# A diffusion transformer block: token tiles loaded into slots, small constants issued from GpSimd, projections three tiles behind

## The chip, the core and the metric

The kernel runs on one core of a Trainium2 chip. The metric is the device time of one execution in microseconds (us); lower is better. The engines are TensorE (PE, with its weight loads PEld), VectorE (DVE), ScalarE (ACT), GpSimd (POOL) and SyncE (SP). SP computes nothing: it issues the transfers between the chip's memory and SBUF. Each engine takes its instructions in the order in which they are written for it, and waits at one whose inputs or buffer are not there yet.

## The reference

One block of a diffusion transformer in float32, with 1024 tokens and 256 context tokens of 1024 features. Six modulation vectors come from a condition vector; attention is over a neighbourhood of 8 x 16 tokens of a 16 x 64 grid plus all context tokens. Cut to what runs:

```python
sh1, sc1, g1, sh2, sc2, g2 = adaln(c, w_mod, b_mod)        # silu(c) @ w_mod + b_mod, in six parts
csh1, csc1, ... = adaln(c_ctx, w_mod, b_mod)
h  = modulate(rms_norm(x,  norm1), sh1,  sc1)              # h * (1 + scale) + shift
hc = modulate(rms_norm(ctx, norm1), csh1, csc1)
q = rms_norm(split_heads(h @ w_q), q_gain)
k = rms_norm(split_heads(h @ w_k), k_gain);   v  = split_heads(h @ w_v)
kc = rms_norm(split_heads(hc @ w_k), k_gain); vc = split_heads(hc @ w_v)
y = neighbourhood_attention(q, k, v, kc, vc, rpb) @ w_o
x = x + g1 * y
x = x + g2 * conv_ffn(modulate(rms_norm(x, norm2), sh2, sc2), w_up, conv_w, conv_b, w_down)
```

## The kernel before

All matrix products that matter are done in a split form: each operand is a rounded part (names ending in h) and a remainder (names ending in l), and three matmuls stand for one product. ACT or DVE makes the rounded part, DVE or POOL subtracts to get the remainder.

The tokens are held in ten tiles of 128 rows and 1024 columns (512 KB): tiles 8 and 9 are the context, 0 to 7 the tokens. A token tile takes eight neighbouring rows out of every 64 rows of x. `TORD` is the order 8, 9, 0, 1, ... 7.

The start, which the change is about, has these steps.

- **Modulation (L240 to L270).** Four segments of w_mod, for scale and shift of the first norm, come as 16 pieces of 512 KB (`mraw`, `load_m`). ACT rounds each (`mh`, L246), DVE makes the remainder (`ml`, L247), PE multiplies (`pm`, L257 and L258). After four pieces ACT copies the sum out (`mrow`, L262), and PE turns it into columns with the small constant `comb` (`pc`, L264). After the eighth piece DVE makes the scale `s1` (L267, L268), after the sixteenth the shift `b1` (L270), with the constants `bcol` and `n1c`.
- **Loads of tokens (`load_x`).** They go into four buffers named `pt`, of which three first hold pieces of w_mod and which the attention uses later. So a fifth tile is loaded only when an earlier one has been transposed.
- **Per tile, `stats_x`:** ACT squares the rows and sums them (L155; the squares themselves are put into `htl`, where nobody reads them), DVE and POOL make the inverse root (`ss`, L156 and L157), DVE scales the tile (L176).
- **Per tile, `transpose_x`:** PE transposes eight blocks of 128 x 128 into PSUM (L182, three buffers), DVE and ACT apply scale and shift to four blocks each (`hv`, L189 and L191), ACT makes `hth` (L193), and DVE or POOL `htl` (L194).
- **Weights of the first pair of heads (`load_w`, `prep_w`):** four transfers `wr` of 384 KB, eight casts `wh` on DVE (L144), eight remainders `wl` on POOL (L147).
- **Projections (`qkv_gen`, L301, L303, L305):** 24 matmuls per tile into one of two PSUM buffers `pq`. The rows are then squared and normalised (L322 to L325) and copied out as `v`, `q` and `kn` (L329 to L340). The `kn` instruction is the last reader of the buffer; the tile after next waits for it.

The later parts of the modulation vectors are computed a little at a time by DVE from transfers `mr` of 128 KB with two buffers (`macc`, L469 and L471), beside the attention of eight pairs of heads. Then follow the output projection and the feed-forward part.

What sets the order: the program is written in the order that the code shows, and a scheduler then lists the instructions of each engine in an order of its own making, with its own estimate of durations. The order of the code decides which of several ready instructions comes first. `AHEAD` in the loop of L549 says by how many tiles the projections follow the transpositions in the code.

All transfers issued by SP share eight completion counters in turn. A transfer is issued only when the one eight places earlier has landed.

`big` is a region of slots under tags; the order list of L118 says which slots hold `hth` and `htl` of which tile.

## Time and profile before

| | us |
|---|---|
| time, median of 3 runs | 1489.94 (1489.22 to 1491.38) |
| profiled execution: span from the first to the last instruction (no other time is listed for it) | 1491.8 |
| PE busy | 1386.5 (93%) |
| DVE busy | 1208.1 (81%) |
| POOL busy | 805.7 (54%) |
| ACT busy | 738.1 (49%) |

The span of the profiled execution is 1.9 us above the median of the runs. In the rows of the profile, each instruction has its start and duration, its engine, its line, what it writes and reads, and in brackets the idle time of its engine before it and what ended that. Rows by group give a count, the sum and the mean of the durations, then the idle time ahead of the group. A row in order of time may merge several equal instructions (x4). A row named SPq is the issue of a transfer, not the transfer.

### The profile page before, as it was taken

What the parts mean: (1) busy time and instruction counts of PE and PEld (TensorE: products, weight loads), DVE (VectorE), ACT (ScalarE), POOL (GpSimd) and SP (SyncE); (2) the same over time, 40 slices, a digit from 0 to 9 for tenths busy, and PEclk for the clock granted to TensorE, in tenths of its full rate; (3) what the DMA queues carried; (4) which work ended last, traced back from release to release, by engine and by line L of the source; (5) the groups of instructions that cost most, each with busy time, mean ns of one, the idle gap of its engine ahead of it and who ended that gap; (6) DMA issues with size and microseconds to landing.
All of it is one profiled execution on the core that took longest, in us unless ns stands there. A gap on an engine that the chain in (4) does not pass through costs nothing.

```text
span 1491.8 us, 22077 instructions
## 1 busy us (share of the span) xinstructions
PE 1386.5 (93%) x7396; PEld 1200.0 (80%) x7396; DVE 1208.1 (81%) x2392; ACT 738.1 (49%) x1601; POOL 805.7 (54%) x672
## 2 busy tenths in 40 slices
PE   6689999999999999999996999999999987898998
PEld 2589889898989899888885777888888865686887
DVE  6778878888888878866589889788877779988884
ACT  6575645555565656645465434344343334244541
POOL 1455544545454546744368545555545568474872
PEclk9899999999999999999997999999999998899999
DMA  9612221313131202262132132233332347433343
GB/s 315 161 37 60 64 87 55 92 51 103 49 101 45 77 14 73 69 152 76 50 129 99 64 108 101 96 106 106 107 106 99 106 137 286 155 100 127 110 131 105
DMA packets 84827, 153.27 MB, mean 103 GB/s; under 512 B 9945, under 2 KB 49001, under 8 KB 84713
## 3 DMA queue, kind: packets, MB, share of 16 engines
q1 hardware_dynamic: 84712, 151.86, 32.7%
q8 instruction: 58, 0.95, 0.3%
q14 instruction: 57, 0.46, 0.1%
HBM read 119.05 MB, written 32.78 MB: 102 GB/s over the span
## 4 chain that ended last, share of the span: by engine, by line
PE 60%; DVE 20%; DMA 7%; POOL 5%; issue 4%; ACT 3%; SPq 0%; DVEq 0%; POOLq 0%; ACTq 0%
PE pg L740 8%; PE pa L740 7%; PE sw L740 6%; PE pq L301 5%; PE pq L303 5%; PE pq L305 5%; DMA mr<-in_w_mod_dram 2%; DVE y L787 2%; DVE p L410 2%; POOL u L688 2%; PE s L398 2%; PE po L448 2%; PE po L449 2%; PE py L525 2%; PE py L526 2%
## 5 line engine op out<-in xcount | busy, mean ns | idle before, releaser
L688 POOL TENSOR_TENSOR u<-ur,u 128x512 fp32r<-128x512 f32 x154 | 231.9, 1519 | 176.8 <-ACT u L687 175.1
L417 POOL TENSOR_TENSOR p<-p,m 128x640 f32<-128x640 f32 (+1 forms) x128 | 157.3, 1230 | 157.0 <-DVE m L413 116.0
L301 PE MATMUL pq<-wh,hth 128*128 128x384 f32 (+1 forms) x640 | 219.7, 343 | 17.1 <-DVE kn L340 15.3
L305 PE MATMUL pq<-wh,htl 128*128 128x384 f32 (+1 forms) x640 | 215.2, 336 | 2.4 <-DVE htl L194 1.4
L303 PE MATMUL pq<-wl,hth 128*128 128x384 f32 (+1 forms) x640 | 215.0, 336 | 0.5 <-POOL wl L147 0.5
L687 ACT ACTIVATE u<-ur 128x512 fp32r<-128x512 f32 x154 | 93.9, 628 | 116.1 <-PE sw L740 45.4
L412 ACT ACTIVATE p<-p,m 128x640 f32<-128x640 f32 (+1 forms) x128 | 102.9, 804 | 84.3 <-DVE m L410 75.2
L301 PEld LDWEIGHTS pq<-wh,hth 128*128 128x128 f32 x640 | 124.8, 195 | 23.1 <-DVE kn L340 9.2
L325 POOL TENSOR_TENSOR qss<-qss,mhalf 128x4 f32<-128x4 f32 (+1 forms) x80 | 79.9, 999 | 97.0 <-DVE qss L324 82.8
L305 PEld LDWEIGHTS pq<-wh,htl 128*128 128x128 f32 x640 | 124.7, 195 | 3.2 <-DVE htl L194 3.2
L303 PEld LDWEIGHTS pq<-wl,hth 128*128 128x128 f32 x640 | 124.8, 195 | 1.6 <-issue 0.9
L787 DVE SCALAR_TENSOR_TENSOR y<-g,cw,y 128x896 f32<-128x896 f32 (+1 forms) x132 | 102.8, 842 | 19.2 <-ACT y L781 19.1
L449 PE MATMUL po<-pt,v 128*128 128x256 f32 x352 | 93.3, 293 | 2.1 <-DVE pt L437 2.1
L448 PE MATMUL po<-pt,v 128*128 128x256 f32 x352 | 93.8, 289 | 0.1
L895 ACT ACTIVATE db<-dr 128x512 fp32r<-128x512 f32 x77 | 47.4, 629 | 87.3 <-PE dx L911 55.7
L871 POOL TENSOR_TENSOR da<-da 128x512 fp32r<-128x512 f32 x44 | 74.9, 1725 | 27.4 <-ACT da L870 27.4
L896 POOL TENSOR_TENSOR db<-dr,db 128x512 fp32r<-128x512 f32 x44 | 64.9, 1494 | 45.6 <-ACT db L895 34.3
L410 DVE CUSTOM_DVE_ANT_0 p<-s,bias 128x640 f32<-128x640 f32 x96 | 78.3, 816 | 9.5 <-PE s L399 8.9
L436 ACT ACTIVATE pt<-pl 128x384 fp32r<-128x384 f32 (+1 forms) x128 | 58.0, 461 | 47.6 <-PE pl L429 46.6
L471 DVE SCALAR_TENSOR_TENSOR macc<-mr,cs,macc 128x256 f32<-128x256 f32 x112 | 65.0, 581 | 13.9 <-DMA mr<-in_w_mod_dram 13.0
L437 DVE TENSOR_TENSOR pt<-pl,pt 128x384 fp32r<-128x384 f32 (+1 forms) x128 | 65.4, 516 | 6.7 <-ACT pt L436 6.2
L449 PEld LDWEIGHTS po<-pt,v 128*128 128x128 f32 x352 | 66.6, 189 | 4.0 <-DVE pt L437 3.4
(258 smaller groups left out, 4184.3 us busy)
## 6 DMA issues: line engine op xcount, KB each, us to landing
ur<-in_w_up_dram SPq DMA_DIRECT2D x44, 512.0 KB
da<-act_dram SPq DMA_DIRECT2D x77, 256.0 KB
mr<-in_w_mod_dram SPq DMA_DIRECT2D x128, 128.0 KB
dr<-in_w_down_dram SPq DMA_DIRECT2D x22, 512.0 KB
wraw<-in_w_qkv_dram SPq DMA_DIRECT2D x56, 192.0 KB
mraw<-in_w_mod_dram SPq DMA_DIRECT2D x16, 512.0 KB
act_dram<-sa SPq DMA_DIRECT2D x11, 512.0 KB
act_dram<-y SPq DMA_DIRECT2D x11, 512.0 KB
```

What stands on the lines that cost most here:

```text
L301: PE.matmul(pq[:, c0:], hth[t][:, k, :], wh[:, c0:], start=(k == 0), stop=False)
L303: PE.matmul(pq[:, c0:], hth[t][:, k, :], wl[:, c0:], start=False, stop=False)
L305: PE.matmul(pq[:, c0:], htl[t][:, k, :], wh[:, c0:], start=False, stop=(k == KC - 1))
L410: DVE.tensor_tensor_reduce(out=dst, in0=src, in1=bb, scale=1.0, scalar=3e38, op0=ALU.add, op1=ALU.min, accum_out=m[:, 0:1])
L412: ACT.activation(w[:, :n], w[:, :n], AF.Exp, bias=m[:, 0:1], scale=-1.0, accum_out=m[:, 1:2])
L417: POOL.tensor_tensor(w[:, :n], w[:, :n], m[:, 2:3].broadcast_to([P, n]), ALU.mult)
L448: PE.matmul(po, v, th[:, j].rearrange("p a b -> p (a b)"), start=(m == 0), stop=False)
L449: PE.matmul(po, v, tl[:, j].rearrange("p a b -> p (a b)"), start=False, stop=(m == len(blks) - 1))
L687: ACT.activation(s[:, 0], r[op], AF.Copy)
L688: POOL.tensor_tensor(s[:, 1], r[op], f(s[:, 0]), ALU.subtract)
L740: PE.matmul(bank, a, b, start=(start and k == 0 and n == 0), stop=(k == 3 and n == 2), skip_group_check=True)
L787: DVE.scalar_tensor_tensor(o, i, w, o, ALU.mult, ALU.add)
```

## The change

- All ten token tiles get a slot of their own in `big` (`xraw`), where later `hth` or `htl` of some tile is put. `load_x` no longer uses the `pt` buffers. A fourth piece of w_mod takes the free `pt` buffer (`PTM`).
- The loads are placed earlier in the code: the first behind eight pieces of w_mod, the second behind twelve, the other eight in the loop over the last eight pieces.
- The squares of `stats_x` go into a PSUM tile, `sqj`, in the banks that the scores `s` use later.
- The first two `stats_x` calls move from the steps 13 and 14 of the modulation to the steps 11 and 13.
- The seven small constants are issued by GpSimd, ahead of the first pieces of w_mod, where SP issued them behind eleven.
- `AHEAD` is 3 instead of 1.

Comments that the diff drops are left out below.

```diff
-AHEAD = 1
+AHEAD = 3
@@ order of the slots
+    xraw = {t: slot(order[2 * i + 1], f"x{t}", F32) for i, t in enumerate(TORD)}
     for i, t in enumerate(TORD):
         hth[t] = slot(order[2 * i], f"hth{t}", shape=(P, KC, P))
         htl[t] = slot(order[2 * i + 1], f"htl{t}", shape=(P, KC, P))
@@ load_x, stats_x
+    sqj = ps.tile([P, D], F32, tag="s", bufs=1, name="sqj")
     def load_x(t):
-        xt = sa.tile([P, D], F32, tag="pt", bufs=4, name=f"xt{t}")
+        xt = xraw[t]
...
-        norm_rows(xin[t], htl[t].rearrange("p a b -> p (a b)"), ss, t in SQD)
+        norm_rows(xin[t], sqj, ss, t in SQD)
@@ modulation
-        MB, PTM = 8, (8, 9, 10)
+        MB, PTM = 8, (8, 9, 10, 11)
...
+        comb_sb = const.tile([4, 2], F32, name="comb_sb")
+        POOL.dma_start(out=comb_sb, in_=comb)
...
         for i in range(MB):
             load_m(i)
         load_x(TORD[0])
         for i in range(MB, AH):
             load_m(i)
-        comb_sb = const.tile([4, 2], F32, name="comb_sb")
-        SP.dma_start(out=comb_sb, in_=comb)
...
+        load_x(TORD[1])
...
-                if i in PTM:
-                    load_x(TORD[1 + i - PTM[0]])
+                if 8 <= i < 16:
+                    load_x(TORD[i - 6])
...
-                if i in (13, 14):
-                    stats_x(TORD[i - 13])
+                if i in (11, 13):
+                    stats_x(TORD[(i - 11) // 2])
@@ the loop over the tiles
         transpose_x(t)
-        if i + 4 < NT:
-            load_x(TORD[i + 4])
         if i + 3 < NT:
             stats_x(TORD[i + 3])
```

SP's queue from the fifth-to-last piece of w_mod on shows the move of the loads (mraw are pieces of w_mod, xt and x the token tiles, wr the first weights). Before:

```order
L209 DMA mraw_168<-in_w_mod_dram 128x2x512
...
L209 DMA mraw_215<-in_w_mod_dram 128x2x512
L213 DMA wr_0_225<-in_w_qkv_dram 128x2x384
L213 DMA wr_1_243<-in_w_qkv_dram 128x2x384
L213 DMA wr_2_261<-in_w_qkv_dram 128x2x384
L170 DMA xt_298<-in_ctxt_dram 128x1024
L168 DMA xt_308<-in_x_dram 128x1x1024
L168 DMA xt_318<-in_x_dram 128x1x1024
L168 DMA xt_427<-in_x_dram 128x1x1024
L213 DMA wr_3_288<-in_w_qkv_dram 128x2x384
```

And now, from the fourth-to-last piece on:

```order
L212 DMA mraw_181<-in_w_mod_dram 128x2x512
L212 DMA mraw_191<-in_w_mod_dram 128x2x512
L171 DMA x_92<-in_x_dram 128x1x1024
L171 DMA x_93<-in_x_dram 128x1x1024
L212 DMA mraw_201<-in_w_mod_dram 128x2x512
L171 DMA x_94<-in_x_dram 128x1x1024
L171 DMA x_95<-in_x_dram 128x1x1024
L212 DMA mraw_211<-in_w_mod_dram 128x2x512
L171 DMA x_96<-in_x_dram 128x1x1024
L171 DMA x_97<-in_x_dram 128x1x1024
L216 DMA wr_0_228<-in_w_qkv_dram 128x2x384
L171 DMA x_98<-in_x_dram 128x1x1024
```

Then follow wr_1, x_99, wr_2 and wr_3. Four token tiles now stand ahead of the last piece of w_mod, six ahead of the first weights, eight ahead of the last two.

ACT's queue around the last mrow (mh is the rounded piece of w_mod, the rows of L155 and L156 are squares of a token tile). Before, the last mrow and the first hth:

```order
L246 ACTIVATE mh_373<-mraw_215 128x1024
L262 ACTIVATE mrow_381<-pm_338 4x512
L155 ACTIVATE htl_93,ss_368<-xt_298 128x1024
L155 ACTIVATE htl_95,ss_398<-xt_308 128x1024
L191 ACTIVATE hv_1_420<-pt_1_415,b_80,s_79 128x128 x4
L155 ACTIVATE htl_97,ss_429<-xt_318 128x1024
L193 ACTIVATE hth_90<-hv_0_408 128x512
```

Now:

```order
L250 ACTIVATE mh_385<-mraw_211 128x1024
L156 ACTIVATE sqj,ss_527<-x_96 128x1024
L156 ACTIVATE sqj,ss_599<-x_97 128x1024
L266 ACTIVATE mrow_394<-pm_352 4x512
L156 ACTIVATE sqj,ss_666<-x_98 128x1024
L194 ACTIVATE hv_1_433<-pt_1_428,b_80,s_79 128x128 x4
L156 ACTIVATE sqj,ss_745<-x_99 128x1024
L196 ACTIVATE hth_100<-hv_1_433 128x512
```

The squares of the fifth and sixth token tiles (x_96 and x_97) stand ahead of the last mrow, and those of the seventh and eighth (x_98 and x_99) ahead of the first hth.

DVE's queue ahead of the first kn, which frees the first buffer pq (pq_8) for the first token tile. Before:

```order
L189 TENSOR_SCALAR hv_0_582<-pt_0_577,s_79,b_80 128x128
L323 TENSOR_REDUCE qss_8_491<-qsq_8_490 128x2
...
L469 TENSOR_SCALAR macc_1186<-mr_0_1187,cs 128x256
L156 TENSOR_SCALAR ss_603<-ss_603 128x1
L471 SCALAR_TENSOR_TENSOR macc_1186<-mr_1_1251,cs,macc_1186 128x256
L194 TENSOR_TENSOR htl_97<-hv_0_582,hth_96 128x512
...
L340 TENSOR_TENSOR kn_4_502<-pq_8_465,qss_8_491 128x128
```

Now:

```order
L192 TENSOR_SCALAR hv_0_647<-pt_0_642,s_79,b_80 128x128 x4
L327 TENSOR_REDUCE qss_8_558<-qsq_8_557 128x2
...
L473 TENSOR_SCALAR macc_1059<-mr_0_1060,cs 128x256
L328 TENSOR_SCALAR qss_8_558<-qss_8_558 128x2
L475 SCALAR_TENSOR_TENSOR macc_1059<-mr_1_1115,cs,macc_1059 128x256
L197 TENSOR_TENSOR htl_111<-hv_0_647,hth_110 128x512
...
L344 TENSOR_TENSOR kn_4_569<-pq_8_532,qss_8_558 128x128
```

The kn of the first context tile stood behind the scale and shift of four tiles (up to hv_0_582, token tile 1) and now stands behind that of six (up to hv_0_647, token tile 3) and behind two more macc.

More of the change, by code (lines that the diff above doesn't have):

```diff
@@ L215, in load_w @@
                 prep_w(0, 2 * i + k, raw[:, k, :])
+        comb_sb = const.tile([4, 2], F32, name="comb_sb")
+        POOL.dma_start(out=comb_sb, in_=comb)
+        bcol = const.tile([P, 48], F32, name="bcol")
+        POOL.dma_start(out=bcol, in_=b_col)
+        n1c = const.tile([P, KC], F32, name="n1c")
+        POOL.dma_start(out=n1c, in_=n1)
+        n2c = const.tile([P, KC], F32, name="n2c")
+        POOL.dma_start(out=n2c, in_=n2)
+        gain_sb = const.tile([P, 2], F32, name="gain_sb")
+        POOL.dma_start(out=gain_sb, in_=gains)
+        cw = const.tile([P, NF, 3], F32, name="cw")
+        POOL.dma_start(out=cw, in_=conv_w)
+        cb = const.tile([P, NF], F32, name="cb")
+        POOL.dma_start(out=cb, in_=conv_b)
         for i in range(MB):
@@ L221, in block_kernel @@
             load_m(i)
-        comb_sb = const.tile([4, 2], F32, name="comb_sb")
-        SP.dma_start(out=comb_sb, in_=comb)
-        bcol = const.tile([P, 48], F32, name="bcol")
-        SP.dma_start(out=bcol, in_=b_col)
-        n1c = const.tile([P, KC], F32, name="n1c")
-        SP.dma_start(out=n1c, in_=n1)
-        n2c = const.tile([P, KC], F32, name="n2c")
-        SP.dma_start(out=n2c, in_=n2)
-        gain_sb = const.tile([P, 2], F32, name="gain_sb")
-        SP.dma_start(out=gain_sb, in_=gains)
-        cw = const.tile([P, NF, 3], F32, name="cw")
-        SP.dma_start(out=cw, in_=conv_w)
-        cb = const.tile([P, NF], F32, name="cb")
-        SP.dma_start(out=cb, in_=conv_b)
+        load_x(TORD[1])
         qg = const.tile([P, 1], F32, name="qg")
```

## The prediction

> **What bounds the kernel now.** The page comes first: PE is busy for 93% of the span, but not in its first two slices of 37 us each. So the second view is the table by stage of the first 100 us.
>
> ```profile
> PE   6689999999999999999996999999999987898998
> ...
> 0.00:20.00 20.00, 10.58 (x33) 2.43 (x33) 11.28 (x15) 12.86 (x15) 1.33 (x9) 1.00 0.91 319
> 20.00:40.00 20.00, 13.30 (x71) 6.77 (x71) 16.55 (x26) 11.58 (x17) 7.95 (x8) 0.95 0.96 299
> 40.00:60.00 20.00, 11.18 (x72) 10.21 (x72) 15.70 (x36) 14.01 (x35) 10.76 (x14) 0.84 0.85 191
> 60.00:80.00 20.00, 15.53 (x84) 15.15 (x85) 14.24 (x40) 10.53 (x26) 5.91 (x6) 0.87 0.39 103
> 80.00:100.00 20.00, 17.98 (x116) 17.37 (x115) 15.75 (x49) 12.32 (x36) 10.54 (x15) 1.00 0.00 2
> ```
>
> The columns are PE, PEld, DVE, ACT, POOL, the granted PE clock, DMA share and GB/s. For 60 us the DMA engines are 85 to 96% busy while PE works little more than half the time; from 80 us on PE is the bound. The third view, PE's order of time, shows where the projections (L301) stood still:
>
> ```profile
> 40.55 2.82 PE L182 MATMUL pt<-ident,xt 128*128 128x128 f32 x12 [3.97 <-DVE xt L176]
> 43.03 0.56 PE L301 MATMUL pq<-wh,hth 128*128 128x256 f32 x1
> ...
> 61.31 0.66 PE L301 MATMUL pq<-wh,hth 128*128 128x384 f32 x1 [7.19 <-DVE kn L340]
> ...
> 76.85 0.41 PE L301 MATMUL pq<-wh,hth 128*128 128x384 f32 x1 [3.16 <-DVE kn L340]
> ```
>
> The two context tiles are projected from 43.03, the first token tile from 61.31, the third from 76.85. Ahead of the later kn stands a late square of a token tile, by ACT's order of time:
>
> ```profile
> 5.22 1.06 ACT L246 ACTIVATE mh<-mraw 128x1024 fp32r<-128x1024 f32 x1 [2.65 <-DMA mraw<-in_w_mod_dram]
> ...
> 34.89 0.59 ACT L262 ACTIVATE mrow<-pm 4x512 f32<-4x512 f32 x1 [2.74 <-PE pm L258]
> ...
> 67.76 0.38 ACT L322 ACTIVATE qsq<-pq 128x256 f32<-128x256 f32 x1 [5.59 <-PE pq L305]
> ...
> 74.66 1.06 ACT L155 ACTIVATE htl<-xt 128x1024 fp32r<-128x1024 f32 x1 [2.53 <-DMA xt<-in_x_dram]
> ...
> 99.42 0.38 ACT L322 ACTIVATE qsq<-pq 128x256 f32<-128x256 f32 x1 [0.58 <-PE pq L305]
> ...
> 104.62 0.38 ACT L322 ACTIVATE qsq<-pq 128x256 f32<-128x256 f32 x1 [1.04 <-PE pq L305]
> ```
>
> Each L322 starts when a tile's projection ends: the first token tile ends at 67.76, the sixth and seventh at 99.42 and 104.62, so the steady pace is 5.20 us a tile.
>
> **The change part by part: the transfers.** SP's order of time, a row of POOL's and the traffic set the price of one transfer. The second fence is 0 to 43 us in 40 slices of 1.075 us, the third 650 to 672 us, where the same array x is read again.
>
> ```profile
> 10.73 0.34 SPq L223 DMA_DIRECT2D comb_sb<-in_comb_dram  x1
> 12.08 0.37 SPq L225 DMA_DIRECT2D bcol<-in_b_col_dram  x1
> ...
> 20.32 2.60 SPq L209 DMA_DIRECT2D mraw<-in_w_mod_dram  x5
> 23.02 1.47 SPq L213 DMA_DIRECT2D wr<-in_w_qkv_dram  x3
> 24.59 0.41 SPq L170 DMA_DIRECT2D xt<-in_ctxt_dram  x1
> 25.61 3.24 SPq L168 DMA_DIRECT2D xt<-in_x_dram  x3
> 29.68 0.38 SPq L213 DMA_DIRECT2D wr<-in_w_qkv_dram  x1
> ...
> 18.95 0.56 POOL L157 TENSOR_TENSOR ss<-ss,mhalf 128x1 f32<-128x1 f32 x1 [17.61 <-DVE ss L156]
> ```
> ```profile
> GB/s 0 8 112 305 402 372 393 404 396 392 383 387 398 398 392 391 381 351 69 21 162 379 404 404 398 394 379 377 372 402 400 251 232 240 232 232 236 236 108 14
> ```
> ```profile
> GB/s 305 305 231 246 238 246 238 261 246 238 238 238 238 253 238 261 233 253 281 290 268 238 246 283 223 246 231 246 238 248 291 259 276 156 30 0 67 209 305 320
> ```
>
> SP's issues come 1.35 us apart, each behind a landing: 512 KB of w_mod per 1.35 us (390 GB/s). The seven constants each took such a turn, and the hole in the traffic behind them goes away (69, 21 and 162 GB/s in three slices: 2.4 us of traffic are missing). POOL, idle for 17.61 us up to 18.95, now issues them. The slices fall from 400 to about 237 GB/s at 33.3 us. By the bytes issued ahead, that is where the three loads from x begin, and the later row repeats 238 for x1<-in_x. A token tile of 512 KB thus costs 2.2 us, against 1.35 us for a context tile of the same size. From above: from 29.68 to the landing of the last wr at 43.03 (DVE's cast of it starts at 43.05, a row below) pass 13.35 us for four wr (1.0 us each at 390), one context tile and three token tiles, which leaves 2.67 us a token tile. I take 2.3, near the slices, since the other figure holds all landing delays.
>
> The Trainium skill, "DMA: Bandwidth & Descriptors", section Latency and other measured facts, says that rows at large powers of two in HBM cut a copy's rate, to 207 GB/s at a 512 KiB pitch; x's tiles take 8 rows out of every 64. The drop to 238 agrees in kind; by 207 a tile would cost 2.5 us (estimate) and the sum below would end 1.2 us later.
>
> The program after the change issues the eight token tiles among w_mod's last pieces and the four wr. The first piece of w_mod lands at 5.22. Up to the sixth token tile follow 15 more pieces, 2 context tiles and 6 token tiles: 5.22 + 17 x 1.35 + 6 x 2.3 = 42.0. Two wr and two more tiles later the last tile is there, 42.0 + 2.0 + 4.6 = 48.6, and the last wr at 50.6. Before, that wr landed at 43.03: **the weights come 7.6 us later, the last token tile some 25 us earlier** (its square waited until 74.66).
>
> **Who waits for it.** ACT and DVE work in their written order. ACT's squares of the fifth and sixth token tiles now stand ahead of the last mrow (L262), so mrow waits for 42.0 where it ran at 34.89. On POOL, the power for the sixth tile stands behind wl of the first wr (43.0). The shift b1 on DVE stands behind that tile's scaling: 43.0 + cast 0.36 + wl 1.21 + power 0.56 + scaling 0.82 + 0.16 = 46.1, by rows above and below. Before it was:
>
> ```profile
> 37.38 0.16 DVE L270 TENSOR_TENSOR b<-pc,bcol 128x16 f32<-128x16 f32 x1
> ...
> 43.05 0.36 DVE L144 CAST wh<-wr 128x384 fp32r<-128x384 f32 x1 [1.32 <-DMA wr<-in_w_qkv_dram]
> ...
> 47.96 1.36 DVE L189 TENSOR_SCALAR hv<-pt,s,b 128x128 f32<-128x128 f32 x4
> 49.23 0.68 DVE L194 TENSOR_TENSOR htl<-hv,hth 128x512 fp32r<-128x512 f32 x1
> ```
>
> No tile can be modulated before b1, so all of that starts 8.7 us later. Then DVE has a queue ahead of kn, which frees the bank for the first token tile. The costs by group, 15 to 110 us:
>
> ```profile
> L189 DVE TENSOR_SCALAR hv<-pt,s,b 128x128 f32<-128x128 f32 x40 | 14.5, 403 | 1.1 <-PE pt L182 1.0
> L194 DVE TENSOR_TENSOR htl<-hv,hth 128x512 fp32r<-128x512 f32 x14 | 10.8, 774 | 1.4 <-ACT hth L193 1.3
> L176 DVE TENSOR_SCALAR xt<-xt,ss 128x1024 f32<-128x1024 f32 x10 | 8.2, 816 | 2.2 <-POOL ss L157 2.2
> L147 POOL TENSOR_TENSOR wl<-wr,wh 128x384 fp32r<-128x384 f32 x8 | 9.6, 1213 | 13.9 <-DVE wh L144 13.9
> L144 DVE CAST wh<-wr 128x384 fp32r<-128x384 f32 x8 | 5.4, 716 | 1.3 <-DMA wr<-in_w_qkv_dram 1.3
> L471 DVE SCALAR_TENSOR_TENSOR macc<-mr,cs,macc 128x256 f32<-128x256 f32 x7 | 3.4, 483 | 3.0 <-DMA mr<-in_w_mod_dram 2.9
> ```
>
> Between b1 and that kn stand 24 hv, 10 htl, 6 wh, 2 scalings and 4 macc: 24 x 0.403 + 10 x 0.774 + 6 x 0.716 + 2 x 0.816 + 4 x 0.45 = 25.1 us; with ten short ones (0.15 to 0.28 each in the same view, 2.3 in all) 27.4. Neighbours overlap by 0.08 us (four hv took 1.27, from 47.96 to 49.23, not 1.61), 56 times: 22.9 us. The first token tile starts at 46.1 + 22.9 = **69.0, 7.7 us later than 61.31**. As before, PE has run dry by then, and I let that tile take 67.76 - 61.31 = 6.45 us again, to 75.45. PE's rows give the rest:
>
> ```profile
> 70.06 0.33 PE L301 MATMUL pq<-wh,hth 128*128 128x384 f32 x1
> ...
> 70.58 0.33 PE L301 MATMUL pq<-wh,hth 128*128 128x384 f32 x1
> ```
>
> Three matmuls from one L301 to the next take 0.52 us, a tile's 24 take 4.2, and the 1.0 that is left of 5.20 is the eight transpositions beside them.
>
> **What is given back.** By 69.0 six tiles are transposed and all are scaled, and no load is outstanding that a projection needs; the two later stalls of before have no cause left. The next four tiles, with one transposition each, take 5.2 us: 75.45 + 20.8 = 96.25 for the fifth. The sixth needs only the four transpositions of q: 96.25 + 4.2 + 0.5 = 100.95. The seventh, with two score steps that now stand ahead of it and inside it (four matmuls of 256 to 384 columns each, 0.6), ends at 100.95 + 4.2 + 1.2 = 106.35. Before, the seventh ended at 104.62 with no score step done; with two it would be 105.8. **The sum is +0.5 us:** 7.7 lost to the later start, 7.2 won back. From there both programs hold the same PE work, and past the third pair of heads the same order.
>
> The rest costs nothing: squares go into a PSUM bank instead of htl (1.06 us each, ACT has gaps), and the memsets of make_pt find POOL idle. No POOL-issued load is in the trace. It costs nothing if it is earlier than SP's issues from 10.73 on, and the time by which it passes 46.1 if b1 has to wait for bcol; I take nothing, as POOL can start at once.
>
> Against the profiled execution: span 1491.8 + 0.5 = 1492.3. The median of the runs is 1489.9, 1.9 below that span, so I predict **1490.4 us**.
>
> **Rivals.** *Faster: the token tiles come at w_mod's pace.* Then the sixth lands at 5.22 + 23 x 1.35 = 36.3, b1 is at 40.4, the first token tile at 63.3, 5.7 us earlier than in the sum: 1484.7. For it speaks that context tiles of the same size took 1.35; against it the 238 at two places. A milder form has DVE's queue free of collisions (cast 0.28, htl 0.60, hv 0.32 apart): about 20 us, 1487.5.
>
> *Slower: DVE and POOL hold each other up.* The queue ahead of kn runs beside eight wl, six powers and the bias on POOL, denser than before. Rows for it:
>
> ```profile
> 33.81 3.58 DVE L144 CAST wh<-wr 128x384 fp32r<-128x384 f32 x4
> ...
> 45.33 1.40 DVE L176 TENSOR_SCALAR xt<-xt,ss 128x1024 f32<-128x1024 f32 x1
> ```
>
> Four casts took 3.58 us instead of 1.1 beside wl, a scaling 1.40 instead of 0.75. If the eight casts and scalings and half of the ten htl lose 0.6 us each, 7.8 us, of which my means hold 3.3 (casts at 0.716 instead of 0.36, htl at 0.774 instead of 0.68), the first tile starts at 73.5 and the time is 1494.9. It decides when DVE needs over 25.5 us from b1 to kn. The Trainium skill, "SBUF — State Buffer", section Who interferes with whom, says that whichever of the two takes the shared ports first holds them for its whole instruction. These rows agree.
>
> *No change in order.* That the scheduler undid the move is excluded by the order it wrote; no chance.
>
> **How the numbers follow.** About 0.2%, 3 us, can be told from no change in a measurement of this kernel. The forecast (within 3 us) has 0.40; its own range is 1487 to 1493.5. Faster holds 0.33: 0.15 for the full rival, the rest for a shorter queue. Slower holds 0.27: collisions 0.19, token tiles at 2.67 us each (the sixth at 44.2, +2.2 us) together with a somewhat longer queue 0.08. The range 1482 to 1497 leaves out under 2 in 10.
>
> **What would show it.** In the changed profile: traffic near 238 GB/s whenever token tiles move, from about 27 us on; the last wr at 50 to 53 us; the last mrow not before 42; b1 near 46; PE's first token projection near 69 behind DVE kn, and no stall over 2 us between it and 105. A first token projection before 65 or after 73 makes the forecast wrong, as does a token tile that lands within 1.5 us of the one ahead.

## The result and the profile after

The changed kernel is slower. Its four runs beside four of the kernel before gave 1501.4 us against 1489.6 us, a ratio of 1.0083 (95% interval 1.0060 to 1.0107). Six more, in another session, gave 1501.6 against 1491.4 us, 1.0076 (1.0058 to 1.0095). So the change costs 10 to 12 us, where the prediction had +0.5 us and a range up to 1497 us.

The table by stage of the changed kernel, with the columns of the prediction's first fence:

```profile
0.00:20.00 20.00, 11.48 (x40) 3.31 (x40) 10.83 (x14) 12.28 (x14) 5.05 (x16) 1.00 0.91 315
20.00:40.00 20.00, 12.04 (x58) 5.29 (x56) 12.84 (x20) 12.92 (x19) 3.77 (x13) 0.91 1.05 293
40.00:60.00 20.00, 11.42 (x45) 8.83 (x46) 14.81 (x35) 13.54 (x28) 10.75 (x12) 0.50 0.91 241
60.00:80.00 20.00, 12.99 (x83) 12.64 (x83) 15.21 (x38) 8.89 (x26) 9.88 (x12) 0.83 0.18 54
80.00:100.00 20.00, 19.55 (x125) 19.16 (x124) 15.76 (x49) 14.24 (x39) 8.92 (x8) 1.00 0.04 11
```

From 40 to 60 us PE made 45 instructions where it made 72 before, at a granted clock of 0.50 (0.84 before), and the transfers moved 241 GB/s with their engines 91% busy. From 80 us on PE is better filled than before (19.55 against 17.98 us): the later stalls are gone. The places that set this, in the orders of time of ACT, DVE and PE:

```profile
38.67 1.03 ACT L156 ACTIVATE sqj<-x 128x1024 f32<-128x1024 f32 x1 [1.57 <-DMA x<-in_x_dram]
40.99 1.06 ACT L250 ACTIVATE mh<-mraw 128x1024 fp32r<-128x1024 f32 x1 [1.18 <-DMA mraw<-in_w_mod_dram]
42.97 1.03 ACT L156 ACTIVATE sqj<-x 128x1024 f32<-128x1024 f32 x1 [0.92 <-DMA x<-in_x_dram]
44.97 1.03 ACT L156 ACTIVATE sqj<-x 128x1024 f32<-128x1024 f32 x1 [0.86 <-DMA x<-in_x_dram]
46.02 0.57 ACT L266 ACTIVATE mrow<-pm 4x512 f32<-4x512 f32 x1
...
46.64 0.36 DVE L145 CAST wh<-wr 128x384 fp32r<-128x384 f32 x1 [0.86 <-DMA wr<-in_w_qkv_dram]
48.72 1.48 DVE L179 TENSOR_SCALAR x<-x,ss 128x1024 f32<-128x1024 f32 x1 [1.39 <-POOL ss L158]
50.13 0.16 DVE L274 TENSOR_TENSOR b<-pc,bcol 128x16 f32<-128x16 f32 x1
72.79 0.28 DVE L344 TENSOR_TENSOR kn<-pq,qss 128x128 f32<-128x128 f32 x1
...
73.21 0.66 PE L305 MATMUL pq<-wh,hth 128*128 128x384 f32 x1 [7.00 <-DVE kn L344]
86.04 0.41 PE L305 MATMUL pq<-wh,hth 128*128 128x384 f32 x1 [0.45 <-DVE kn L344]
```

ACT waits for each landing in turn: the fourth token tile at 38.67, the last piece of w_mod at 40.99, the fifth and sixth token tile at 42.97 and 44.97. Then comes the last mrow at 46.02 (34.89 before), the first wr for DVE's cast at 46.64, b1 at 50.13 (37.38) and the first token projection at 73.21 (61.31).

### The profile page after: what moved, and what is told of

Same layout as the page of the kernel before. It is cut to its first block, busy times and chain, and to the rows that moved or that the text cites. A ratio compares the mean times of both kernels' runs of the same rounds, so it can differ in the third digit from the quotient of the medians.

```text
span 1500.6 us, 22109 instructions
## 1 busy us (share of the span) xinstructions
PE 1389.4 (93%) x7396; PEld 1200.2 (80%) x7396; DVE 1202.0 (80%) x2392; ACT 736.5 (49%) x1601; POOL 806.3 (54%) x679
## 5 line engine op out<-in xcount | busy, mean ns | idle before, releaser
L898 POOL TENSOR_TENSOR db<-dr,db 128x512 fp32r<-128x512 f32 x44 | 65.7, 1512 | 48.7 <-ACT db L897 37.4
L897 ACT ACTIVATE db<-dr 128x512 fp32r<-128x512 f32 x77 | 47.5, 630 | 86.5 <-PE dx L913 52.6
L873 POOL TENSOR_TENSOR da<-da 128x512 fp32r<-128x512 f32 x44 | 70.5, 1623 | 27.2 <-ACT da L872 20.8
L440 ACT ACTIVATE pt<-pl 128x384 fp32r<-128x384 f32 (+1 forms) x128 | 58.1, 461 | 47.6 <-PE pl L433 46.7
```

## The experiments

The numbers at a glance. The ratio is to the kernel before in the same session, whose medians were 1489.9, 1491.4 and 1490.5 us; where two kernels of different sessions are compared below, the difference of their ratios is taken, times 1490 us. b1 and the first token projection are read from each kernel's profile, in us.

| kernel | what it is | median, us | ratio (95%) | b1 | first token projection |
|---|---|---|---|---|---|
| before | three profiles | | | 37.4, 37.4, 37.6 | 61.3, 58.5, 60.3 |
| after, after2 | the change, two profiles | 1501.4, 1501.6 | 1.0083, 1.0076 | 50.1, 51.7 | 73.2, 74.8 |
| e1_const | before, constants on POOL | 1491.2 | 1.0005 (0.9995 to 1.0016) | 38.3 | 58.1 |
| e5_ahead3 | before, AHEAD = 3 | 1501.2 | 1.0073 (1.0051 to 1.0094) | 37.6 | 59.3 |
| e2_ahead1 | after, AHEAD = 1 | 1494.8 | 1.0041 (1.0025 to 1.0057) | 51.3 | 68.1 |
| e4_rows | after, x in contiguous rows | 1494.7 | 1.0039 (1.0023 to 1.0056) | 45.6 | 67.1 |
| e6_sq | after, two squares behind b1 | 1502.8 | 1.0081 (1.0058 to 1.0104) | 47.5 | 75.3 |
| e3_behind | after, token loads behind the weights | 1493.0 | 1.0018 (1.0003 to 1.0033) | 40.9 | 61.9 |
| e7_act | e3_behind, weight casts on ACT | 1491.6 | 1.0004 (0.9990 to 1.0017) | 36.6 | 51.9 |
| e8_act1 | e7_act, AHEAD = 1 | 1486.7 | 0.9980 (0.9966 to 0.9994) | 37.1 | 52.2 |
| e9_late | after, one subtraction at 815 us moved | 1501.7 | 1.0081 (1.0059 to 1.0102) | 50.9 | 74.3 |

### The parts alone: constants, and AHEAD

e1_const: the kernel before with the block of seven small loads moved.

```diff
+        comb_sb = const.tile([4, 2], F32, name="comb_sb")
+        POOL.dma_start(out=comb_sb, in_=comb)
...
         for i in range(MB):
             load_m(i)
...
-        comb_sb = const.tile([4, 2], F32, name="comb_sb")
-        SP.dma_start(out=comb_sb, in_=comb)
...
```

> The kernel before, with one part of the change: the seven constants are issued from POOL at the start, all else as before. Theory (the loss comes from the token tiles' transfers ahead of b1): this part does no harm. The hole of 2.4 us in the traffic behind the constants goes, the last mrow comes at about 33 instead of 34.89, the first token projection at 59.5 to 61.3; the later stalls on kn stay, so the time is 0 to 2 us under the kernel before. Rival (loads issued from POOL cost something): something waits for a constant, or POOL's first powers come later; 1494 or more.

In the time as the theory had it: 1.0005, no difference. The constants do no harm. In its steps the theory failed. The hole in the traffic went (three slices near 9 us fell to 320 to 340 GB/s in its place), but the last mrow came at 35.71, not at about 33, and b1 at 38.3, no earlier than before:

```profile
35.71 0.59 ACT L262 ACTIVATE mrow<-pm 4x512 f32<-4x512 f32 x1 [1.73 <-PE pm L258]
```

mrow waits for PE, and the last pieces ahead of it wait for engines and not for transfers: ACT's last mh for PE (0.93 us), and DVE's last `ml` takes 1.73 us beside wl on POOL (1.23 us for most others). So earlier landings alone did not bring an earlier b1. At 58.1 the first token projection lies just ahead of what the kernel before shows in its three profiles, and in the time nothing of it can be told.

e5_ahead3: the kernel before, only

```diff
-AHEAD = 1
+AHEAD = 3
```

> The kernel before, with one part of the change: AHEAD = 3, the first projections three tiles behind the transposes; loads, buffers and constants as before. In the kernel e2_ahead1 taking this part out of the change brought the time from 1501.6 to 1494.8 us. Theory (three more modulated tiles in DVE's queue ahead of the first kn cost 5 us by themselves, wherever b1 is): the first token projection at 65 to 68 instead of 61 to 65, time 3 to 7 us over the kernel before, 1494 to 1498. Rival (it costs only together with the late b1 and the late weights of the changed kernel): within 2 us of the kernel before.

The time came out even higher than the theory had it, 11 us over the kernel before, but not for its reason: the first token projection did not come later.

```profile
37.60 0.15 DVE L270 TENSOR_TENSOR b<-pc,bcol 128x16 f32<-128x16 f32 x1
58.84 0.28 DVE L340 TENSOR_TENSOR kn<-pq,qss 128x128 f32<-128x128 f32 x1
78.19 0.66 PE L301 MATMUL pq<-wh,hth 128*128 128x384 f32 x1 [6.01 <-DVE v L330]
```

b1 to kn took 21.2 us, as in the kernel before; the stall went to the third token tile (6.0 us at 78.19). This execution was 5 us faster than the median of its kernel, so the kernel was profiled once more.

> The kernel before with AHEAD = 3 once more, for a second profile. Its first profiled execution took 1496.2 us, 5 us under the median of its six runs (1501.2), so where this part loses its 10.7 us could not be read there: at 400 us it stood 4.2 us behind the second profile of the kernel before, at 900 us 8.4, at the end 9.4. Theory (AHEAD = 3 costs in the start-up, by the longer queue ahead of the kn): 6 us or more behind at 400 us and 3 to 5 more by the end. Rival (its cost lies after the attention, in another order at the start of the up projection): 4 us or less behind at 400 us and 6 or more gathered behind 800.

That execution took 1496.6 us, again less than the other runs of the kernel (1499.7 to 1504.0). Against the second profile of the kernel before it stood some 6 us behind at 400 us and 9.9 at the end, which is near the theory; against the third, a slower execution of the same session, 2.1 and 3.2, which is near neither. Where a run of 1501 us loses its 11 us has not been seen.

e2_ahead1: the changed kernel with `AHEAD = 1`.

> The changed kernel with the first projections one tile behind the transposes again (AHEAD = 1); token tiles and constants as in the change. Between b1 and the first kn DVE then has 16 hv and 8 htl in place of 24 and 10. Theory (the loss comes from the transfers): b1 stays at 50, the first token projection comes about 4 us earlier than 73.2, but the modulations taken out of the queue come back ahead of the next kn; the end is within 2 us of the changed kernel, 1499 to 1503. Rival (the loss is the queue of three tiles ahead of kn): the first token projection before 68 and no new stalls; 1493 or less.

The theory failed here. The time fell by 5 to 6 us, not by less than 2. DVE's order of time shows the shorter queue:

```profile
51.30 0.16 DVE L274 TENSOR_TENSOR b<-pc,bcol 128x16 f32<-128x16 f32 x1
67.61 0.29 DVE L344 TENSOR_TENSOR kn<-pq,qss 128x128 f32<-128x128 f32 x1
```

b1 is as late as in the changed kernel, but kn follows it after 16.3 us instead of 22.7, and the seventh token tile's projection ends at 107.3 instead of 111.1 (the latter with two score steps, 1.2 us by the prediction's working). So AHEAD = 3 is a cause of its own beside the loads; how much of it comes by the queue ahead of kn is taken up below.

### What the token loads cost: e4_rows

```diff
-            SP.dma_start(out=xt, in_=xv[t])
+            SP.dma_start(out=xt, in_=x[t * P:(t + 1) * P, :])
```

> The changed kernel, but each token tile is read from 128 rows of x that lie one behind the other, in place of 8 rows out of every 64; all issues stay at their places. The tokens are thereby permuted, so this kernel does not compute the reference's output. Theory (the strided rows slow all that is mixed with them to some 245 GB/s): traffic stays near 390 GB/s to the end of the loads, a token tile lands 1.35 us behind the one ahead, the sixth at about 36.3 (44.9 in the changed kernel), b1 at 40 to 42, the first token projection at 62 to 65, and the time is 7 to 10 us under the changed kernel, 1491 to 1494. Rival (the order on the queue, not the rows, sets the pace): traffic still falls to about 245, time 1499 or more.

The traffic from 23 to 63 us in 40 slices, first of the changed kernel, then of e4_rows:

```profile
GB/s 389 393 352 221 258 256 234 244 330 223 258 262 238 244 268 250 246 246 240 231 259 250 239 224 272 244 230 242 276 372 371 357 282 281 193 6 0 0 0 0
```
```profile
GB/s 391 389 408 410 395 404 401 410 406 401 393 399 412 389 397 398 379 372 369 383 363 190 87 291 208 268 32 0 0 0 0 0 0 0 0 8 0 0 0 0
```

With contiguous rows nothing falls: 390 GB/s to the end of the loads at 44 us. So it is the spacing of x's rows that lowers the pace from 390 to 245 GB/s, and it does so for all that is mixed with them: in the changed kernel the slices stay near 245 from 26 to 52 us, though w_mod's last pieces and the four wr pass in that time too. The order of the issues is the same in both. The Trainium skill, "DMA: Bandwidth & Descriptors", section Latency and other measured facts, has such a fall for pitches of 512 KiB and more; these runs show it for eight rows of 4 KB out of every 256 KB, and show that neighbours on the queue pay too.

The time fell by 5.5 to 6.5 us, a little less than the 7 to 10 expected. b1 came later than expected, 45.6 instead of 40 to 42:

```profile
36.53 1.06 ACT L250 ACTIVATE mh<-mraw 128x1024 fp32r<-128x1024 f32 x1 [0.48 <-DMA mraw<-in_w_mod_dram]
...
42.15 0.59 ACT L266 ACTIVATE mrow<-pm 4x512 f32<-4x512 f32 x1 [1.89 <-PE pm L262]
...
45.55 0.16 DVE L274 TENSOR_TENSOR b<-pc,bcol 128x16 f32<-128x16 f32 x1
...
67.13 0.66 PE L305 MATMUL pq<-wh,hth 128*128 128x384 f32 x1 [7.55 <-DVE kn L344]
```

The last w_mod piece is still 5.6 us ahead of the last mrow. Here mrow no longer waits for squares but for PE, whose matmul waits for the remainder `ml` behind the scalings of two token tiles on DVE. The rows that it reads are other tokens than the tile's, so e4_rows computes another result than the reference and is of use for its times alone.

### Which wait holds b1: e6_sq

In the changed kernel two squares stand ahead of the last mrow on ACT. Here they wait for b1:

```diff
+        if t in TORD[6:8]:
+            POOL.tensor_copy(ss, b1[:, 0, 0:1])
         norm_rows(xin[t], sqj, ss, t in SQD)
```

> The changed kernel, but the squares of the fifth and sixth token tiles wait for b1 (POOL copies a column of b1 into the sum that the square then writes), so that ACT's last mrow and DVE's b1 no longer stand behind these two tiles. Loads and their order stay. Theory (two parts of the delay of b1: the last w_mod piece lands late, 41.0, and mrow waits for the two tiles behind it): the last piece stays at 41, the last mrow comes at 43 to 44 instead of 46.0, b1 at 45 to 47 instead of 50.1, the first token projection at 68 to 71, time 2 to 5 us under the changed kernel. Rival (only the late landing counts, the squares fill time that is lost anyway): b1 at 49 or later, no difference.

b1 came 2.6 us earlier, just short of what the theory had, and it brought nothing: 1502.8 us.

```profile
46.97 0.63 DVE L145 CAST wh<-wr 128x384 fp32r<-128x384 f32 x2 [3.97 <-DMA wr<-in_w_qkv_dram]
47.52 0.17 DVE L276 TENSOR_TENSOR b<-pc,bcol 128x16 f32<-128x16 f32 x1
51.07 0.36 DVE L145 CAST wh<-wr 128x384 fp32r<-128x384 f32 x1 [3.38 <-DMA wr<-in_w_qkv_dram]
51.34 1.04 DVE L194 TENSOR_SCALAR hv<-pt,s,b 128x128 f32<-128x128 f32 x3
```

Behind b1 stands the cast of the next weights, which land at 51: the first modulation `hv` starts at 51.34, later than in the changed kernel (50.67). The late loads hold DVE at two places, and taking away the first shows the second.

### The loads behind the weights: e3_behind, e7_act, e8_act1

e3_behind issues the eight token tiles behind the last w_mod piece and the four wr.

```diff
-    def load_x(t):
+    def load_x(t, after=None):
         xt = xraw[t]
+        if after is not None:
+            POOL.tensor_copy(xt[:, 0:1], after)
...
-                if 8 <= i < 16:
-                    load_x(TORD[i - 6])
+                    for t in (TORD[2:] if i == 8 else []):
+                        load_x(t, f(mh)[:, 0, 0:1])
```

> The changed kernel, but each token tile's load waits for a copy of one column (POOL) that is made from the ninth cast piece of w_mod, so SP issues all eight behind the last w_mod piece and the four wr; ACT's order then has the last mrow ahead of all token squares. Theory (the transfers ahead of b1 are the loss): the last w_mod piece lands at 5.2 + 17 x 1.35 = 28, the last wr near 32, b1 at 33 to 36 (50.1 in the changed kernel), the first token projection at 55 to 60 (73.2), and with the later stalls gone the time is 1480 to 1487, faster than both kernels. Rival (the early loads are harmless, the queue ahead of kn and DVE with POOL are the loss): b1 early, but the first token projection still after 66, time 1494 or more.

Some 9 us under the changed kernel, but not under the kernel before; the theory's direction held, its size did not. DVE shows why b1 was not at 33 to 36:

```profile
33.03 1.22 DVE L253 TENSOR_TENSOR ml<-mraw,mh 128x1024 fp32r<-128x1024 f32 x1
34.16 6.77 DVE L145 CAST wh<-wr 128x384 fp32r<-128x384 f32 x7
40.86 0.16 DVE L277 TENSOR_TENSOR b<-pc,bcol 128x16 f32<-128x16 f32 x1
```

Seven casts ahead of b1 took 0.97 us each beside POOL's wl, where one alone takes 0.35. In e7_act ACT makes these casts (`WD, SQD = (), ()` in place of `range(8), ()`).

> As e3_behind (token loads behind w_mod and the four wr), and the eight casts of the first weights go to ACT instead of DVE, since in e3_behind seven of them took 6.8 us on DVE beside wl on POOL and held b1 back to 40.9. Theory (what counts is when b1 comes and what DVE has between it and kn): b1 at 37 to 38, 16 hv, 5 htl and 4 scalings up to the first kn take 12 to 15 us, the first token projection starts at 50 to 56, and the time is 3 to 6 us under e3_behind, 1485 to 1489, at or under the kernel before. Rival (an early start is given back: PE then runs at half clock after its idle time, or the tiles come too late for it): the start-up is 3 us or more shorter at 300 us, but the time is 1490 or more.

b1 and the first token projection came about where the theory had them (36.6 and 51.9), the time at 1491.6 did not: equal to the kernel before. PE's order of time has the rest:

```profile
51.94 0.41 PE L308 MATMUL pq<-wh,hth 128*128 128x384 f32 x1 [0.58 <-DVE kn L347]
62.72 1.11 PE L187 MATMUL pt<-ident,x 128*128 128x128 f32 x4 [5.36 <-DVE hv L194]
74.48 0.44 PE L308 MATMUL pq<-wh,hth 128*128 128x384 f32 x1 [1.55 <-DVE kn L347]
...
58.65 0.75 DVE L181 TENSOR_SCALAR x<-x,ss 128x1024 f32<-128x1024 f32 x1 [0.74 <-POOL ss L158]
60.90 0.48 DVE L478 SCALAR_TENSOR_TENSOR macc<-mr,cs,macc 128x256 f32<-128x256 f32 x1 [1.49 <-DMA mr<-in_w_mod_dram]
61.30 1.36 DVE L194 TENSOR_SCALAR hv<-pt,s,b 128x128 f32<-128x128 f32 x4
```

The first token tile's projection ends at 58.6, 6 to 9 us earlier than in the three profiles of the kernel before; the second one's at 72.8, hardly earlier (76.0, 72.3 and 75.3 there). In the last three rows, DVE's order of time, the queue waits in turn for POOL and for a transfer `mr`, which was issued behind all the token tiles. Part of the early start was given back there, as the rival had it. At 300 us PE stood 4.3 us ahead of the third profile of the kernel before and level with the second, and 2.4 us of that went between 800 and 900 us (see the table under e9_late).

e8_act1 is e7_act with `AHEAD = 1`.

> As e7_act (token loads behind w_mod and the weights, the first weights cast on ACT), with AHEAD = 1. In e7_act the first token projection started at 51.9 but the next tiles stood at 62.7 and 74.5 behind DVE, whose queue waited for w_mod's next pieces and for POOL. Theory (with two tiles fewer modulated ahead of kn the second and third tile come earlier): the first token projection at 48 to 54, the third token tile's end at 72 to 76 (79.1 in e7_act), time 1486 to 1490, at or under the kernel before. Rival (the tiles' modulations are only moved behind kn, as the waits are): the third tile ends at 78 or later, time 1490 or more.

1486.7 us, 3.6 us under e7_act, and the one kernel here that beats both: 0.9980 (0.9966 to 0.9994) of the kernel before, some 3 us. The first token projection is where e7_act had it; the third tile ended at 76.5, just outside the expected 72 to 76, the seventh at 97.3 (104.6, 101.0 and 105.4 in three executions of the kernel before).

### A loss far from the change: e9_late

In both profiles of the changed kernel PE waits 4.2 us for `b5l` at about 825 us, at the start of the up projection; the kernel before waits 2.35 us there, for `b7l`. POOL's, DVE's and PE's order of time, changed kernel (the second line is the view of the tile, with shortest, median and longest duration in ns and the first and last start):

```profile
817.27 7.74 POOL L649 TENSOR_TENSOR b3l<-x,b3h 128x256 fp32r<-128x256 f32 x2
L649 POOL TENSOR_TENSOR b3l<-x,b3h x2: 717/3886/7056, 817.3 to 824.3; 128x256 fp32r<-128x256 f32 x2
...
818.18 0.68 DVE L713 TENSOR_TENSOR w<-x,x 128x512 f32<-128x512 f32 x1
819.39 0.68 DVE L676 TENSOR_TENSOR ur<-ur,ur 128x512 f32<-128x512 f32 x1
...
826.97 0.80 PE L742 MATMUL pg<-b5l,u 128*128 128x512 f32 x1 [4.22 <-POOL b5l L649]
```

And the same work in the kernel before:

```profile
811.86 2.06 POOL L647 TENSOR_TENSOR b3l<-x,b3h 128x256 fp32r<-128x256 f32 x2
...
813.25 1.22 DVE L711 TENSOR_TENSOR w<-x,x 128x512 f32<-128x512 f32 x1
814.39 1.77 DVE L710 TENSOR_TENSOR w<-x 128x512 f32<-128x512 f32 x1
...
821.62 0.50 PE L740 MATMUL sw<-b7l,u 128*128 128x512 f32 x1 [2.35 <-DVE b7l L647]
```

Before, DVE and POOL take turns: DVE's instructions are stretched to 1.2 to 1.8 us, and POOL's two b3l take about 1.0 us each. After, DVE runs nine of 0.68 us and two shorter ones without a gap, from 817.58 to 823.75, and POOL's first b3l ends only when DVE pauses, at 824.33: it took 7.06 us and the second 0.72, together 7.74 us for two that took 2.06, and b5l behind them is late. The scheduler had put one subtraction b4l of DVE ahead of the modulation of the last tile instead of into it, and three matmuls of PE some rows further up: the only rows past the third pair of heads that differ. e9_late puts b4l behind it.

```diff
+                    if t == 7 and k == 2:
+                        ACT.activation(BT[4, "l", 0][:, 0, 2 * P:2 * P + 1], v[:, kk, 0:1], AF.Copy)
+                        split_b(4, *held.pop())
...
-            split_b(4, m, t4)
+            if m == 2:
+                held.append((m, t4))
+            else:
+                split_b(4, m, t4)
```

> The changed kernel, with one place at 815 us put otherwise: in both of its profiles two subtractions b3l on POOL took 7.74 us there (2.06 in the kernel before) while DVE ran one short operation behind the other, and PE then waited 4.2 us for the next b5l. Here one subtraction b4l on DVE stands behind the modulation of the last tile, as in the kernel before, held there by a copy of one column on ACT; all up to 780 us is as in the changed kernel. Theory (the order of DVE at this place, which the change has shifted by some rows, costs 2 to 3 us): b3l back to 2 to 3 us, no wait on b5l over 2 us, time 1498 to 1500. Rival (POOL is late there for another reason, or a wait of the same size takes its place): 1501 or more.

```profile
821.40 2.32 POOL L654 TENSOR_TENSOR b3l<-x,b3h 128x256 fp32r<-128x256 f32 x2
```

At its place it did what the theory said: b3l took 2.32 us and the wait on b5l was gone. The time did not show it, 1501.7 against 1501.6 us, with an interval of 0.2% (3 us) on each; by the time alone the rival's 1501 or more holds. How far the same matmul of PE lies behind the third profile of the kernel before tells more of the place. These are differences of starts in two traces, at matmuls near 800 and 900 us:

```
              at 800 us   at 900 us   gained by the kernel before in between
before           +1.6        +1.7        0.1
before2          -4.3        -4.0        0.3
after            +7.0       +10.0        3.0
after2           +5.2        +8.9        3.7
e3_behind        +0.2        +3.8        3.6
e4_rows          -0.2        +3.3        3.5
e5_again         +2.2        +4.5        2.3
e6_sq            +9.2       +11.7        2.5
e7_act           -4.1        -1.7        2.4
e8_act1          -6.8        -4.3        2.5
e9_late         +11.0       +11.3        0.3
```

Every kernel in this list whose start was changed loses 2.3 to 3.7 us there; three executions of the kernel before, and e9_late, do not. It is not one cause: e3_behind and e5_again have b3l in turns with DVE and lose theirs in a wait of 3.1 us for DVE's `tmp` near 855 us, e7_act and e8_act1 wait 4.0 us for `b7l` instead. e9_late shows the cause for the order of the changed kernel alone. (In e1_const and e2_ahead1 the order of PE differs more at this place, so that their rows cannot be set side by side.) What the profiled execution of e9_late won here it had lost between 250 and 800 us, where PE's order is the same as in the changed kernel: a difference between executions. That the median of its runs is no lower either stays unexplained; that the place costs the change 3 us of time is read from positions in traces and not shown by a time.

### The changed kernel and the kernel before once more

> The changed kernel once more, unchanged, for a second profile and more runs. In the first profile it stood 5.5 us behind the kernel before from the fourth pair of heads to 810 us, and 8.3 to 8.8 us from 845 us on. Theory (the start-up costs 5.5 us for good, the 3 us after 810 us are of that one execution: how the start of the up projection falls on its waits and on the half-clock stretches): the first token projection again at 73, again 4 to 6 us behind at 500 us, but another figure behind 845 us; median 1495 to 1499. Rival (the 3 us belong to the change): the same wait on b5l near 820 us, 8 us behind from 845 us on, median 1500 to 1503.

The second profile had the wait on b5l again (4.2 us, b3l 7.74 us) and the median was 1501.6: the rival was right, the late wait belongs to the change.

> The kernel before once more, for a second profile. Theory (single executions differ by where the half-clock stretches fall): the first token projection again at 61 to 62, start-up within 1 us of the first profile, but 1 to 4 us of difference gathered at other places, above all where the granted clock is halved while PE has work; span 1484 to 1492. Rival (executions of one kernel follow the same course): both profiles within 1 us everywhere.

> The kernel before a third time, for its profile. Its two profiles so far have b1 at 37.4 and the first token projection at 61.3 and 58.5 us, and stand 6 us apart at 300 us. Theory (the sum of the prediction was made against an execution whose start was slow by some 3 us, by collisions of DVE and POOL between b1 and kn): b1 at 37.4 again, the first token projection between 58 and 62, and at 810 to 900 us the same waits as in both (b7l 2.4 us, no b5l). Rival (61.3 is the usual course and 58.5 the exception): 61 or later.

Neither side of the first expectation (before2) held: the executions differ, and the start itself is among the places. b1 to kn took 23.5, 20.7 and 22.2 us in three executions of one kernel. DVE's order of time ahead of kn, first and then second profile:

```profile
57.38 0.35 DVE L469 TENSOR_SCALAR macc<-mr,cs 128x256 f32<-128x256 f32 x1 [1.44 <-DMA mr<-in_w_mod_dram]
58.48 0.48 DVE L471 SCALAR_TENSOR_TENSOR macc<-mr,cs,macc 128x256 f32<-128x256 f32 x1 [0.69 <-DMA mr<-in_w_mod_dram]
```
```profile
55.25 0.35 DVE L469 TENSOR_SCALAR macc<-mr,cs 128x256 f32<-128x256 f32 x1
55.63 0.48 DVE L471 SCALAR_TENSOR_TENSOR macc<-mr,cs,macc 128x256 f32<-128x256 f32 x1
58.04 0.28 DVE L340 TENSOR_TENSOR kn<-pq,qss 128x128 f32<-128x128 f32 x1
```

In the first execution DVE waited 2.1 us for two transfers `mr`, in the third 1.0 us (0.61 and 0.39), in the second not at all. That is most of the spread, so it comes from these transfers, and not from the collisions of DVE and POOL that the theory of before3 named. The execution that the prediction was made against had the longest start of the three, so the gap to a usual execution is some 1 to 3 us more than its profile says.

## Why the prediction was wrong

**Which wait sets the start: right.** The chain of the prediction is the chain of the trace: token tiles among w_mod's last pieces, mrow behind the squares of the fifth and sixth tile, b1 behind their scaling, the DVE queue, kn, the first token projection. Half of its terms came out to a few tenths: b1 to the first token projection 23.1 us (forecast 22.9), the first tile 6.7 (6.45), 4.9 to 5.5 us for each later tile with no stall over 0.5 us, and no harm from the constants.

**The landings: the term that was mis-sized.** The prediction had the sixth token tile at 42.0, the first wr at 43.0 and b1 at 46.1. They came at 44.97, 46.64 and 50.13. So 3.6 of the 4.0 us by which b1 was late are there when the wr lands; the rest is mostly that tile's scaling, 1.48 us beside wl on POOL where the sum had 0.82. The waits for POOL behind it are those of the sum.

The pace of the traffic was not the mistake. The sum gave a token tile 2.3 us and a piece of w_mod 1.35 us also where they are mixed. ACT's rows show 2.3, 2.0 and 2.0 us from landing to landing, whichever array comes: the mixed traffic has one pace, some 245 GB/s. The two pieces of w_mod were too cheap and the six tiles too dear, and that cancels (16.5 us by the sum, 17.1 for 4.2 MB at 245 GB/s), which was luck. What had moved by 42 and by 45 us:

```profile
DMA packets 5871, 12.65 MB, mean 301 GB/s; under 512 B 695, under 2 KB 755, under 8 KB 5870
DMA packets 6214, 13.39 MB, mean 297 GB/s; under 512 B 718, under 2 KB 1001, under 8 KB 6213
```

The 24 loads up to the sixth tile, with the constants, are 12.67 MB. As many bytes had moved at 42.1 us, where the sum had them, but the tile was there for ACT only 2.9 us later, and by then 0.7 MB more had moved, of the loads that SP had issued behind it. What failed is that the sum took a landing for the moment when the bytes ahead of it have moved. The prediction had the other price in hand: 2.67 us a token tile, measured from issue to landing, puts the sixth at 44.2. It was set aside for 2.3 "since the other figure holds all landing delays", and whoever waits for a tile waits for these too. The rival with 2.67 had a chance of 0.08. What makes up the 2.9 us, a slow end of the tile itself or the others' bytes ahead of it, these rows do not separate.

The late b1 brought the first token projection to 73.2 instead of 69.0 (past the prediction's own mark of 73), and the end of the seventh tile to 111.1 instead of 106.35: 4.75 us of the miss. e4_rows shows that the spacing of the rows is worth 5.5 to 6.5 us of the change's cost; that cost was in the sum, at 2.3 us a tile.

**"Past the third pair of heads the same order": wrong.** A few rows at the start of the up projection had moved, in both engines' orders, and I took rows so far from the change for free. The sum had nothing for this. In the two profiles the changed kernel falls 3.0 and 3.7 us further behind between 800 and 900 us; e9_late shows that the wait goes when the order of DVE is put back, though not that the time falls.

**The baseline.** The sum was made against one execution and shifted to the median by its time. But its start was not the usual one (kn 1 to 3 us later than in two others, most of it waits for `mr`), so what the change adds to the start was taken too small by about that. The time of an execution does not say at which place it was slow.

**AHEAD = 3: counted once, and not as a loss.** The prediction had the three modulated tiles in DVE's queue (24 hv, 10 htl) and let them come back as a gain by tiles without stalls. The gain came: the later stalls are gone. Yet undoing AHEAD in the changed kernel wins 5 to 6 us and in e7_act 3.6 us, and adding it to the kernel before loses 11 us. In the changed kernel the longer queue explains 5.1 us at the start of the first token tile (73.2 against 68.1), of which 2.6 are left at the end of the seventh (111.1 less 1.2 against 107.3). What makes up the rest, and the whole of e5_ahead3's loss, stays open.

**The sum of the misses.** Between the two first profiles it closes: spans of 1500.6 and 1491.8 us differ by 8.8 us where the forecast had 0.5, and 4.75 at the start and 3.0 between 800 and 900 us are 7.75 of these 8.3. The medians differ by 11.8 us, 3 us more. The 1 to 3 us of the baseline would fill that; this part is an estimate, since the executions differ at other places too (the table under e9_late has 6 us between two of the kernel before).

What undoing each part wins does not add up to the loss, and need not: rows 6 and AHEAD 5.5 us by the time, the place at 815 us 3 us by positions only, of 10 to 12 us in all. AHEAD = 3 alone costs the kernel before 11 us, and with the loads behind the weights (e3_behind) the kernel that has it is 3 us over the kernel before. No run here has contiguous rows together with AHEAD = 1, so how the parts depend on each other is open.

**The rivals.** The faster one asked for token tiles at w_mod's pace and put b1 at 40.4; e4_rows had that pace, but b1 at 45.6, and was still 1.0039. The slower one, collisions of DVE and POOL, was to decide from 25.5 us between b1 and kn; it was 22.7, so it did not decide there. DVE and POOL did hold each other up at a place that the prediction had not looked at, at 815 us.

## What to carry to other kernels

A transfer is priced by what travels with it: a slow pattern in a queue sets the pace of everything between its first and its last piece, so strided loads belong behind whatever the next stage waits for, not among it (e3_behind: about 9 us). And price it from issue to landing where something waits for it: bytes over pace gave 42.0 here, the landing was at 44.97. Where a scheduler writes the order, compare the whole order, not the stage that was edited: three matmuls and one subtraction some 750 us away brought a new wait of 4.2 us in both profiles of the change. And a sum against one profiled execution inherits how that execution ran; two or three profiles of the kernel before are cheap beside an effect of under 1%.

## What the runs showed of the hardware that was not expected

- Short DVE instructions back to back can shut POOL out: a POOL subtraction of 256 columns that takes 0.7 us alone took 7.06 us while DVE ran nine of 0.68 us and two shorter ones. A slightly other order gave turns, of 1.2 to 1.8 us on DVE and about 1.0 us on POOL. The Trainium skill, "SBUF — State Buffer", section Who interferes with whom, has the one that starts first hold the shared ports for its whole instruction; that POOL may lose many turns in a row was new.
- Token tiles of 8 rows out of 64 moved at some 245 GB/s (most slices 220 to 280), and so did w_mod and weights between them; tiles of contiguous rows at the same places kept 390 GB/s.
- The mean granted PE clock was 0.966 over the six runs of the changed kernel against 0.973 of the kernel before in the same session. In the first profile of the change the clock was halved from 36 to 60 and from 70 to 77 us (38 to 45 and 58 to 65 us before). In the first stretch PE was busy for 13.0 of 23.9 us and then waited 7.0 us for kn, behind a DVE queue without gaps, so there the lower clock was not by itself a cost.
- Loads issued from POOL at the start took POOL 0.53 to 0.72 us each and landed 4.0 to 6.3 us after their issue; nothing waited for them. SP's traffic fell from some 395 to 320 to 340 GB/s in three slices meanwhile (e1_const).
